# Two transformer layers on one core: u at the phase starts worked out by DVE and ACT alone, with other split points, load queues and buffer counts

## The chip, the core and the metric

The kernel runs on one core of a Trainium2 chip. A core has a matmul engine (TensorE, PE in the profile; its weight loads are PEld), a vector engine (DVE), a scalar engine (ACT), a general one (POOL, GpSimd) and a queue engine (SyncE, SP) that issues most of the DMAs. Each runs its own instructions in the order of its program, and they wait for one another through semaphores. The metric is the device time of one execution in microseconds; less is better.

## What is computed

Two layers act on 128 context tokens and 128 latent tokens with the same weights, in float32, at 1024 channels. Each layer has three phases, and each starts with an RMS norm with a modulation (shift, scale) of its own:

```
u = modulate(rms_norm(x, g[0]), sh1, sc1)
x = x + 0.5 * gt1 * swiglu(u, w_ffn1_in, w_ffn1_out)
u = modulate(rms_norm(x, g[1]), sh2, sc2)
y, ctx_out = token_mixer(u, ...)     # z = u @ w_in: attention, Fourier mixing, mLSTM; gates from u; w_out
x = x + gt2 * y
u = modulate(rms_norm(x, g[2]), sh3, sc3)
x = x + 0.5 * gt3 * swiglu(u, w_ffn2_in, w_ffn2_out)
```

The latent tokens' attention also reads cached keys and values (`cache_k`, `cache_v`), and their mLSTM a cached state (`state_C`). A final norm ends the program. Keys, values and states of the context tokens are outputs too.

## The kernel before

The residual lies in SBUF as `xT`, eight blocks of 128 channels, 256 tokens wide (two groups of 128). A product in float32 is made of three products of rounded halves: `mm3` multiplies `whi` by `uh`, `whi` by `ul` and `wlo` by `uh` (the page's lines 168 to 170). So a weight chunk of 1 MB comes by DMA into one of `N_RAW` raw buffers, on SP's queue, and is split into two units: ACT rounds a unit (`whi`, L1493), DVE subtracts (`wlo`, L1494), into one of `N_SPLIT` split buffers. `pump_split(n)` splits up to n units if a split buffer is free. A raw buffer comes free when both its units are split; then `pump_dma` puts the next load on SP's queue, in the order of the program. A unit of eight blocks is 24 matmuls of 256 columns.

The order of every engine is the order in which the Python program emits instructions (a manual schedule): `steps` are run one after the other, each with its units, then `pump_split`, then what was put into `late`.

Where a phase begins (`first`, used by the mixers and by all FFNs but the very first), four units are multiplied by y = x times scale, which needs no statistics; 1 / rms multiplies the result afterwards. Beside the eight blocks of these products run: `stats` (four small products that sum squares, then the variance on DVE and its power on POOL, L473 and L475), `diag` (1 / rms on a diagonal, `dg`, DVE and ACT), `spread` (a product that spreads it to all partitions, copied to `bcs`), and `apply`, which makes u block by block for all later products:

```
v = vs[k] = t2([P, 256], "v")
(po if k else ve).tensor_mul(v, xT[:, k, :], self.bc)
ac.activation(v[:, G[0]], v[:, G[0]], AF.Identity, scale=self.scale[:, k, 0:1], ...)
ve.tensor_scalar(v[:, G[1]], v[:, G[1]], self.scale[:, k, 1:2], ...)
if k > 0:
    hilo(vs.pop(k - 1), *uk(k - 1))
```

So v is x / rms (POOL for blocks 1 to 7, DVE for block 0, L495); one group is scaled by ACT (L496), the other by DVE (L498); `hilo` rounds the block on ACT (`uh`, L179) and subtracts on DVE (`ul`, L180). `held` has the last two blocks of y, and `warm` loads an ACT table where the phase is an FFN (L520). The four products end in `done`, which reads their PSUM tiles.

In a mixer `loads2` follows directly: it loads cached keys and values (`ckv`) and states (`C0`) on POOL's queue (L695 to L698). The lanes, generators that the steps advance, make attention, gates, mLSTM and Fourier mixing beside the products. The attention lane transposes the cached keys on PE in the middle of the third unit multiplied by u, and swaps parts of q by DMAs on SP's queue (`kl<-q`, L814).

Of the kernel before, what the change touches and what calls it, by code (L numbers as in the profile page):

```python
# [11 lines left out]
F32R = mybir.dt.float32r  # L12
# [5 lines left out]
P = 128  # L18
# [15 lines left out]
N_RAW = 7  # L34
N_SPLIT = 6
# [6 lines left out]
# modulation vectors that each phase works out: those the vector engine sums first, and the others  # L42
# [37 lines left out]
def _pack(inputs):  # L80
    """Short vectors side by side, 128 wide, and the per-head gate biases and stabilisers."""
# [43 lines left out]
def trunk_kernel(ctx: ExitStack, tc: tile.TileContext, a: dict):  # L125
# [58 lines left out]
    # ---------------------------------------------------------------- small inputs  # L184
# [22 lines left out]
    # ---------------------------------------------------------------- persistent  # L207
# [36 lines left out]
    # ---------------------------------------------------------------- start-up  # L244
# [38 lines left out]
    def busy(n):  # L283
        """Products of nothing, which bring the tensor engine to its full clock while it has no data."""
        t = pb([P, 512])
        for _ in range(n):
            mm(t, zeros[:, 0:P], zeros)
# [10 lines left out]
    # ---------------------------------------------------------------- modulation  # L298
    def mod_steps(mods_):
        """Products of some modulation vectors.  # L300

        Four products run side by side: two quarters of the channels, two terms of their sums.
        Vector i takes the rows 2 i and 2 i + 1 of each. The vector engine first sums the channel
        blocks of those of the first list, one term per group, and the products sum its lanes."""
# [88 lines left out]
    # ---------------------------------------------------------------- norms  # L393
    class Norm:
        """Statistics and scaled copies of the residual, block by block.

        y = x * scale goes into the first products of the next phase as it is, with the shift as
        two more columns; 1 / rms multiplies their result. The other products take
        u = y / rms + shift."""

        def __init__(self, scale, shift):
            self.scale, self.shift = scale, shift
            self.y = self.sum = self.last = None
            self.ys = {}
# [58 lines left out]
        def natural(self, x):  # L463
            """Statistics of rows that lie one token to a partition."""
# [23 lines left out]
        def apply(self):  # L488
            U.h = [blk([P, 4, 256], f"uh{i}", F32R) for i in range(2)]
            U.l = [blk([P, 4, 256], f"ul{i}", F32R) for i in range(2)]  # L490
            vs = {}
            for k in range(KD + 1):
                if k < KD:
                    v = vs[k] = t2([P, 256], "v")
                    (po if k else ve).tensor_mul(v, xT[:, k, :], self.bc)  # L495
# [21 lines left out]
    def warm(func):  # L517
        """Has the scalar engine fetch the table of a function before it is needed."""
        if func is not None:
            ac.preload_act_table(func)  # L520

    def first(norm, us, done, func=None):
        """The first four products of a phase, which run while the norm is worked out."""
        ps = first_tiles()
        for k in range(KD):
            first_k(norm.yk, k, us, ps)
            if k == 0:
                norm.stats()
                warm(func)
                held.pop(0)()  # L530
                norm.diag()
                while held:
                    held.pop(0)()
                pump_split(1)
            if k == 1:
                norm.spread()
        norm.apply()
        pump_split(1)
# [7 lines left out]
    def scaled(norm, p_):  # L546
        """A product of y from PSUM times 1 / rms, and its shift, one column per group."""
# [39 lines left out]
    # ---------------------------------------------------------------- FFN  # L587
# [95 lines left out]
    # ---------------------------------------------------------------- mixer  # L683
    def add_mixer(l, norm, norm_next, mods_):
# [7 lines left out]
        def loads2():  # L692
            ac.preload_act_table_set("natural_log_exp_and_others")
            M["ck"] = blk([P, 2, H, P], "ckv")
            po.dma_start(out=M["ck"][:, 0], in_=a["cache_k"][0, l].rearrange("h s d -> s h d"))  # L695
            po.dma_start(out=M["ck"][:, 1], in_=a["cache_v"][0, l].rearrange("h s d -> s h d"))
            M["C0"] = blk([P, 2, H, P], "C0")
            po.dma_start(out=M["C0"], in_=a["state_C"][0, l].rearrange("d h v k -> v d h k"))  # L698
# [95 lines left out]
        # ---- attention  # L794
        def attn_lane():
# [14 lines left out]
            def swap(src):  # L810
                """The halves of each component change places by 32 partitions."""
# [102 lines left out]
            # context  # L914
# [18 lines left out]
            # latent  # L933
# [27 lines left out]
        # ---- Fourier mixing  # L961
        def four_lane():
            """Real input: tokens t and T - t share the cosine part and differ in the sine's sign."""
# [33 lines left out]
        # ---- mLSTM  # L997
        def gate_lane():
# [52 lines left out]
            # rows 4 to 7 of each direction repeat the heads, and carry what rounding leaves of nM  # L1051
# [38 lines left out]
        def mlstm_lane():  # L1090
# [16 lines left out]
            # latent part that comes from the initial memory  # L1107
# [14 lines left out]
            # context state  # L1122
# [97 lines left out]
        # ---- branch products, gates, merge  # L1220
# [83 lines left out]
    def spread_into(lo, hi, mods_):  # L1304
        """Inserts the steps of modulation vectors evenly between two places of the program."""
# [6 lines left out]
    # ---------------------------------------------------------------- program  # L1312
# [6 lines left out]
    def begin(plain_done, st1):  # L1319
        """The first modulation comes one channel block at a time, and the first products with it.  # L1320

        Returns the units of the second pair, of which the first half is used here."""
# [237 lines left out]
```

## Time and profile before

| | before |
|---|---|
| median of 3 runs | 1375.77 us (1375.19 to 1377.95) |
| span of the profiled execution | 1375.9 us |
| PE busy | 1351.3 us, 98% |
| DVE busy | 915.0 us, 67% |
| ACT busy | 682.3 us, 50% |
| POOL busy | 113.0 us, 8% |
| moved from HBM | 297.80 MB, 219 GB/s over the span |
| mean granted clock of TensorE | 0.990 |

The page shows no other time of the profiled execution than its span, which is within the range of the runs. Busy times of engines overlap. A matmul's record lasts some 0.28 us and the next starts about 0.12 us later, so PE's pace is read from start to start. The granted clock is 1.00 for 2.4 GHz and 0.50 for 1.2 GHz.

### The profile page before, as it was taken

Reading aid. Unit: us, or ns where it says so; the run is one execution under the profiler, and the core shown is the slowest. Engines: PE = TensorE matmul, PEld = TensorE weight load, DVE = VectorE, ACT = ScalarE, POOL = GpSimd, SP = SyncE. Lnnn points to the kernel's source line nnn. Section 1 sums busy time; section 2 is a strip of 40 time slices with the busy share of each in tenths; the row PEclk is TensorE's granted clock in tenths of the full one; section 3 lists DMA queues with packets and bytes.
Section 4 is the critical chain, followed back from the end, with each engine's and each line's share of the span. In section 5 each row is a group of like instructions: output and inputs, shape, how many; then the busy total and the mean of one; then the engine's idle time right before and its main releaser. Section 6 shows DMA issues by size and latency. Waiting matters only on the chain.

```text
span 1375.9 us, 26101 instructions
## 1 busy us (share of the span) xinstructions
PE 1351.3 (98%) x10915; PEld 1268.7 (92%) x10916; DVE 915.0 (67%) x1440; ACT 682.3 (50%) x1096; POOL 113.0 (8%) x138
## 2 busy tenths in 40 slices
PE   6999999999999999999999999999999999999998
PEld 4999899888998999999998999998899899999998
DVE  4576755876557589666568666667665668887653
ACT  4544444666544466444455444546564445744442
POOL 2000001300000030000020000130000001200000
PEclk8999999999999999999999999999999999999999
DMA  9999856564468847886639876748445895487520
GB/s 293 333 345 340 260 174 213 159 195 138 157 238 298 272 154 267 300 269 212 206 124 321 305 257 197 204 130 241 154 137 195 297 304 186 147 264 233 192 85 31
DMA packets 247526, 303.68 MB, mean 221 GB/s; under 512 B 5537, under 2 KB 212657, under 8 KB 247409
## 3 DMA queue, kind: packets, MB, share of 16 engines
q1 hardware_dynamic: 245728, 296.98, 66.4%
q0 software_dynamic: 1680, 5.05, 1.1%
q8 instruction: 85, 1.39, 0.4%
q14 instruction: 33, 0.26, 0.1%
HBM read 297.80 MB, written 3.15 MB: 219 GB/s over the span
## 4 chain that ended last, share of the span: by engine, by line
PE 90%; DVE 6%; ACT 2%; DMA 1%; issue 1%; SPq 1%; POOL 0%; ACTq 0%; DVEq 0%
PE pm L168 26%; PE pm L170 25%; PE pm L169 25%; PE pd L165 5%; PE pb L165 2%; DVE wlo L1494 2%; DVE v L498 2%; DVE ul L180 1%; PE pm L752 1%; PE pm L754 1%; PE pm L753 1%; ACT whi L1493 1%; PE pa L165 1%; DMA raw<-w_ada 1%; PE pa L173 1%
## 5 line engine op out<-in xcount | busy, mean ns | idle before, releaser
L1494 DVE TENSOR_TENSOR wlo<-raw,whi 128x1024 fp32r<-128x1024 f32 (+1 forms) x424 | 507.3, 1204 | 326.4 <-ACT whi L1493 316.8
L1493 ACT CAST whi<-raw 128x1024 fp32r<-128x1024 f32 (+1 forms) x424 | 433.9, 1031 | 364.3 <-PE pm L169 253.4
L168 PE MATMUL pm<-uh,whi 128*128 128x256 f32 x1928 | 554.7, 288 | 0.0
L169 PE MATMUL pm<-ul,whi 128*128 128x256 f32 x1928 | 546.8, 284 | 1.7 <-DVE v L498 1.3
L170 PE MATMUL pm<-uh,wlo 128*128 128x256 f32 x1928 | 544.7, 283 | 3.2 <-DVE wlo L1494 3.2
L168 PEld LDWEIGHTS pm<-uh,whi 128*128 128x128 f32 x1928 | 366.8, 190 | 23.7 <-ACT whi L1493 9.1
L170 PEld LDWEIGHTS pm<-uh,wlo 128*128 128x128 f32 x1928 | 366.4, 190 | 4.4 <-DVE wlo L1494 4.4
L169 PEld LDWEIGHTS pm<-ul,whi 128*128 128x128 f32 x1928 | 366.2, 190 | 3.8 <-DVE v L498 1.7
L169 PE MATMUL pm<-hl,whi 128*128 128x256 f32 x704 | 197.9, 281 | 0.0
L168 PE MATMUL pm<-hh,whi 128*128 128x256 f32 x704 | 197.5, 281 | 0.0
L170 PE MATMUL pm<-hh,wlo 128*128 128x256 f32 x704 | 197.5, 281 | 0.0
L168 PEld LDWEIGHTS pm<-hh,whi 128*128 128x128 f32 x704 | 132.8, 189 | 0.0
L170 PEld LDWEIGHTS pm<-hh,wlo 128*128 128x128 f32 x704 | 132.7, 189 | 0.0
L169 PEld LDWEIGHTS pm<-hl,whi 128*128 128x128 f32 x704 | 132.6, 188 | 0.0
L423 POOL TENSOR_TENSOR nsum<-nsum,nsq 128x256 f32<-128x256 f32 x36 | 36.4, 1012 | 833.7 <-ACT nsq L421 833.7
L339 DVE SCALAR_TENSOR_TENSOR acc<-raw,cT,acc 128x512 f32<-128x512 f32 x112 | 78.9, 746 | 0.0
L165 PE MATMUL pd<-raw,cT 128*32 128x512 f32 (+1 forms) x512 | 56.5, 560 | 8.7 <-DMA raw<-w_ada 5.0
L653 ACT ACTIVATE silu<-pm 128x512 f32<-128x512 f32 x39 | 23.3, 597 | 69.5 <-PE pm L170 69.5
L165 PEld LDWEIGHTS pd<-raw,cT 128*32 128x32 f32 x512 | 14.0, 112 | 30.8 <-issue 20.4
L655 DVE TENSOR_TENSOR silu<-silu,pm 128x512 f32<-128x512 f32 x40 | 27.4, 685 | 22.6 <-PE pm L170 22.6
L568 DVE SCALAR_TENSOR_TENSOR xT<-pm,mod,xT 128x128 f32<-128x128 f32 x96 | 28.8, 342 | 18.1 <-PE pm L170 18.0
L1238 ACT ACTIVATE sig<-pm 128x512 f32<-128x512 f32 x24 | 14.4, 598 | 50.3 <-PE pm L170 50.1
(340 smaller groups left out, 1757.8 us busy)
## 6 DMA issues: line engine op xcount, KB each, us to landing
raw<-w_ffn_in SPq DMA_DIRECT2D x88, 1024.0 KB, 7.1
raw<-w_ada SPq DMA_DIRECT2D x64, 1024.0 KB, 6.0
raw<-w_ffn_out SPq DMA_DIRECT2D x32, 1024.0 KB, 7.1
raw<-w_in SPq DMA_DIRECT2D x32, 1024.0 KB, 5.9
raw<-w_branch_gate SPq DMA_DIRECT2D x24, 1024.0 KB, 5.4
raw<-w_ffn_out SPq DMA_DIRECT2D x16, 768.0 KB, 4.8
raw<-w_ada SPq DMA_DIRECT2D x16, 512.0 KB, 7.3
raw<-w_out SPq DMA_DIRECT2D x8, 1024.0 KB, 6.6
```

What stands on the lines that cost most here:

```text
L165: pe.matmul(out, lhsT, rhs, start=start, stop=stop)
L168: pe.matmul(out, sh, mh, start=start, stop=False)
L169: pe.matmul(out, sh, ml, start=False, stop=False)
L170: pe.matmul(out, sl, mh, start=False, stop=stop)
L339: ve.scalar_tensor_tensor(x, w, c, x, op0=ALU.mult, op1=ALU.add)
L423: eng.tensor_add(self.sum, self.sum, sq)
L498: ve.tensor_scalar(v[:, G[1]], v[:, G[1]], self.scale[:, k, 1:2], self.shift[:, k, 1:2], op0=ALU.mult, op1=ALU.add)
L568: ve.scalar_tensor_tensor(xT[:, k, G[g]], ps[:, G[g]], gate[:, k, g:g + 1], xT[:, k, G[g]], op0=ALU.mult, op1=ALU.add)
L653: ac.activation(st["s"], st["a"], AF.Silu)
L655: ve.tensor_mul(st["s"], st["s"], st["g"])
L1493: ac.copy(u.hi, r)
L1494: ve.tensor_sub(u.lo, r, u.hi.bitcast(F32))
```

## The change

- `apply` multiplies by 1 / rms on DVE for all eight blocks, and can be called in two parts: blocks 0 to 4 (with `hilo` up to block 3), then the rest.
- `first` emits `stats` and `diag` after the second block of y products instead of the first, `spread` and `apply` after the third instead of the second and the last. A unit is split ahead of the statistics, and one between the two parts of `apply`.
- The mixers' loads of `ckv` and `C0` are issued by SP instead of POOL.
- `N_SPLIT` is 7 instead of 6, `N_RAW` 6 instead of 7.

```
-N_RAW = 7
-N_SPLIT = 6
+N_RAW = 6
+N_SPLIT = 7
...
-        def apply(self):
-            U.h = [blk([P, 4, 256], f"uh{i}", F32R) for i in range(2)]
-            U.l = [blk([P, 4, 256], f"ul{i}", F32R) for i in range(2)]
-            vs = {}
-            for k in range(KD + 1):
+        def apply(self, k1=KD + 1):
+            if self.at == 0:
+                U.h = [blk([P, 4, 256], f"uh{i}", F32R) for i in range(2)]
+                U.l = [blk([P, 4, 256], f"ul{i}", F32R) for i in range(2)]
+            vs = self.vs
+            ks, self.at = range(self.at, k1), k1
+            for k in ks:
                 if k < KD:
                     v = vs[k] = t2([P, 256], "v")
-                    (po if k else ve).tensor_mul(v, xT[:, k, :], self.bc)
+                    ve.tensor_mul(v, xT[:, k, :], self.bc)
...
             first_k(norm.yk, k, us, ps)
             if k == 0:
-                norm.stats()
                 warm(func)
                 held.pop(0)()
+                pump_split(1)
+            if k == 1:
+                norm.stats()
                 norm.diag()
                 while held:
                     held.pop(0)()
-                pump_split(1)
-            if k == 1:
+            if k == 2:
                 norm.spread()
-        norm.apply()
-        pump_split(1)
+                norm.apply(5)
+                pump_split(1)
+                norm.apply()
+                pump_split(1)
...
-            po.dma_start(out=M["ck"][:, 0], in_=a["cache_k"][0, l].rearrange("h s d -> s h d"))
-            po.dma_start(out=M["ck"][:, 1], in_=a["cache_v"][0, l].rearrange("h s d -> s h d"))
+            nc.sync.dma_start(out=M["ck"][:, 0], in_=a["cache_k"][0, l].rearrange("h s d -> s h d"))
+            nc.sync.dma_start(out=M["ck"][:, 1], in_=a["cache_v"][0, l].rearrange("h s d -> s h d"))
             M["C0"] = blk([P, 2, H, P], "C0")
-            po.dma_start(out=M["C0"], in_=a["state_C"][0, l].rearrange("d h v k -> v d h k"))
+            nc.sync.dma_start(out=M["C0"], in_=a["state_C"][0, l].rearrange("d h v k -> v d h k"))
```

How this moves the instructions, at the start of layer 0's mixer. Numbers behind a name are those of its buffer; lines of the changed kernel are a few higher. DVE before, from the weight split ahead of u on (v_2816 is block 0, v_2820 block 1):

```order
L1494 TENSOR_TENSOR wlo_2721<-raw56_2263,whi_2720 128x1024
L495 TENSOR_TENSOR v_2816<-xT_96,bcs_2738 128x256
L498 TENSOR_SCALAR v_2816<-v_2816,mod0_4_103,mod0_3_102 128x128
L498 TENSOR_SCALAR v_2820<-v_2820,mod0_4_103,mod0_3_102 128x128
L180 TENSOR_TENSOR ul0_2814<-v_2816,uh0_2812 128x256
L498 TENSOR_SCALAR v_2826<-v_2826,mod0_4_103,mod0_3_102 128x128
L180 TENSOR_TENSOR ul0_2814<-v_2820,uh0_2812 128x256
```

DVE in the changed kernel, around the middle of u (v_2782 is block 4, v_2792 block 5):

```order
L498 TENSOR_TENSOR v_2782<-xT_96,bcs_2754 128x256
L501 TENSOR_SCALAR v_2782<-v_2782,mod0_4_103,mod0_3_102 128x128
L180 TENSOR_TENSOR ul0_2758<-v_2776,uh0_2756 128x256
L1500 TENSOR_TENSOR wlo_2789<-raw57_2362,whi_2788 128x1024
L498 TENSOR_TENSOR v_2792<-xT_96,bcs_2754 128x256
L501 TENSOR_SCALAR v_2792<-v_2792,mod0_4_103,mod0_3_102 128x128
L180 TENSOR_TENSOR ul1_2759<-v_2782,uh1_2757 128x256
```

Before, DVE scales and subtracts in turn and multiplies only block 0; now a multiplication stands ahead of each scaling, behind the subtraction of the block before the last, and a `wlo` stands in the middle of u.

ACT before, from the second to last block of y to the copy of 1 / rms (`bcs`):

```order
L435 ACTIVATE y<-xT,mod_4_103 128x128
L179 CAST yh_2103<-y 128x256
L480 ACTIVATE dg<-cst,rstd 128x128
L435 ACTIVATE y<-xT,mod_4_103 128x128
L179 CAST yh_2103<-y 128x256 x2
L1493 CAST whi<-raw_2263 128x1024
L486 COPY bcs<-pb 128x256
```

The same stretch of ACT in the changed kernel:

```order
L435 ACTIVATE y<-xT,mod_4_103 128x128
L179 CAST yh_2107<-y 128x256
L1499 CAST whi<-raw_2291 128x1024
L480 ACTIVATE dg<-cst,rstd 128x128
L435 ACTIVATE y<-xT,mod_4_103 128x128
L179 CAST yh_2107<-y 128x256 x2
L486 COPY bcs<-pb 128x256
```

The weight split has moved from behind the diagonal to ahead of it; on DVE its `wlo` has moved in the same way to a place ahead of the variance. In an FFN the table load stands ahead of all this on ACT, in both kernels.

SP before, where the attention's swap of q comes (`raw` are the weight loads; the loads of `ckv` and `C0` stand on POOL, behind the seven multiplications):

```order
L1471 DMA raw_2868<-w_in 128x8x256
L1471 DMA raw_2878<-w_in 128x8x256
L1471 DMA raw_2913<-w_in 128x8x256
L1471 DMA raw_2993<-w_in 128x4x512
L814 DMA kl<-q 32x4x128 x4
```

SP in the changed kernel:

```order
L1477 DMA raw_2876<-w_in 128x8x256
L1477 DMA raw_2911<-w_in 128x8x256
L701 DMA ckv<-cache_k 128x4x128
L702 DMA ckv<-cache_v 128x4x128
L704 DMA C_2921<-state_C 128x8x128
L1477 DMA raw_2966<-w_in 128x8x256
L1477 DMA raw_3031<-w_in 128x4x512
L820 DMA kl<-q 32x4x128 x4
```

The cached keys, values and states now stand in SP's queue behind `raw_2876`, which waits for the raw buffer of units 7 and 8, and `raw_2911`, which waits for that of units 9 and 10 (the first four units are those of the y products).

## Rows read from the trace of the kernel before

**Rows 1.** Head of the page: the span; engine, busy us, share, instructions.

```profile
span 1375.9 us, 26101 instructions
PE 1351.3 (98%) x10915; PEld 1268.7 (92%) x10916; DVE 915.0 (67%) x1440; ACT 682.3 (50%) x1096; POOL 113.0 (8%) x138
```

**Rows 2.** PE by windows: stretch, length, busy (matmuls), granted clock, DMA share, GB/s.

```profile
720.00:722.00 2.00, 2.00 (x19) 1.00 0.00 0
722.00:724.00 2.00, 1.51 (x11) 1.00 0.03 8
258.00:260.00 2.00, 2.00 (x11) 0.50 0.77 155
262.00:264.00 2.00, 2.00 (x16) 0.84 1.09 350
```

**Rows 3.** Timeline of PE, layer 0's mixer: start, us, instruction, [idle before <-releaser].

```profile
250.69 0.29 PE L168 MATMUL pm<-uh,whi 128*128 128x256 f32 x1
...
257.33 0.58 PE L170 MATMUL pm<-uh,wlo 128*128 128x256 f32 x1 [0.47 <-DVE wlo L1494]
...
263.81 0.60 PE L173 MATMUL pa<-cst,ckv 128*128 128x128 f32 x4
```

**Rows 4.** Timeline of DVE and POOL at the same mixer start.

```profile
244.49 0.96 DVE L495 TENSOR_TENSOR v<-xT,bcs 128x256 f32<-128x256 f32 x1
...
250.43 0.83 POOL L695 DMA_DIRECT2D ckv<-cache_k  x1
...
251.10 1.86 DVE L180 TENSOR_TENSOR ul<-v,uh 128x256 fp32r<-128x256 f32 x1
...
255.09 0.42 DVE L180 TENSOR_TENSOR ul<-v,uh 128x256 fp32r<-128x256 f32 x1 [0.49 <-ACT uh L179]
...
263.51 2.36 DVE L1494 TENSOR_TENSOR wlo<-raw,whi 128x1024 fp32r<-128x1024 f32 x2 [1.08 <-ACT whi L1493]
```

**Rows 5.** Timeline of DVE at the start of layer 1's first FFN.

```profile
709.13 0.16 DVE L473 TENSOR_SCALAR var<-pb 128x2 f32<-128x2 f32 x1 [1.60 <-PE pb L165]
...
712.39 1.23 DVE L1494 TENSOR_TENSOR wlo<-raw,whi 128x1024 fp32r<-128x1024 f32 x1 [0.50 <-ACT whi L1493]
713.53 0.95 DVE L495 TENSOR_TENSOR v<-xT,bcs 128x256 f32<-128x256 f32 x1
...
720.83 0.43 DVE L180 TENSOR_TENSOR ul<-v,uh 128x256 fp32r<-128x256 f32 x1
721.17 0.34 DVE L498 TENSOR_SCALAR v<-v,mod,mod 128x128 f32<-128x128 f32 x1
```

**Rows 6.** Timeline of ACT at the same FFN start.

```profile
708.06 1.28 ACT L520 ACT_TABLE_LOAD   x1
...
711.31 1.05 ACT L1493 CAST whi<-raw 128x1024 fp32r<-128x1024 f32 x1
...
720.01 0.49 ACT L496 ACTIVATE v<-v,mod,mod 128x128 f32<-128x128 f32 x1
720.41 0.39 ACT L179 CAST uh<-v 128x256 fp32r<-128x256 f32 x1
```

**Rows 7.** Timeline of PE at the same FFN start.

```profile
710.86 0.67 PE L165 MATMUL pb<-dg,ones 128*128 128x256 f32 x2 [0.21 <-ACT y L435]
...
720.00 0.28 PE L168 MATMUL pm<-uh,whi 128*128 128x256 f32 x1
...
724.27 0.38 PE L170 MATMUL pm<-uh,wlo 128*128 128x256 f32 x1 [0.76 <-DVE wlo L1494]
```

**Rows 8.** DMA issues of 245 to 275 us: queue, count, KB, us to landing.

```profile
raw<-w_in SPq DMA_DIRECT2D x5, 1024.0 KB, 6.1
...
ckv<-cache_k POOLq DMA_DIRECT2D x1, 256.0 KB, 3.2
...
kl<-q SPq DMA_DIRECT2D x4, 64.0 KB, 5.0
```

**Rows 9.** Timeline of DVE during start-up.

```profile
24.00 2.36 DVE L1494 TENSOR_TENSOR wlo<-raw,whi 128x1024 fp32r<-128x1024 f32 x2 [0.52 <-ACT whi L1493]
```

More of the change, by code (lines that the diff above doesn't have):

```diff
@@ L403, in __init__ @@
             self.y = self.sum = self.last = None
-            self.ys = {}
+            self.ys, self.vs, self.at = {}, {}, 0
         def begin(self):
@@ L533, in first @@
                     held.pop(0)()
+            if k == 2:
+                norm.spread()
+                norm.apply(5)
                 pump_split(1)
-            if k == 1:
-                norm.spread()
-        norm.apply()
-        pump_split(1)
+                norm.apply()
+                pump_split(1)
         def rest():
```

## The prediction

> **What bounds the kernel now.** I read the head of the page first: TensorE (PE) is busy 98% of a span of 1375.9 us [rows 1]. So only PE's gaps can be won back, and whatever makes PE wait longer is paid in full. The profiled execution's span is 0.1 us from the median of the three runs, 1375.77 us, so sums made on the trace carry over unchanged.
>
> Next the timeline of PE where a phase begins. There are five such places that `first` serves: two mixers (near 240 and 909 us) and three FFNs (near 508, 709 and 1177 us). PE runs eight blocks of products of y, which need no statistics, while DVE and ACT work out u; then it turns to products of u. In layer 0's mixer the first product of u starts at 250.69, PE then starves, the second weight's first `wlo` product runs only at 257.33, and PE reaches its look at the cached keys at 263.81 [rows 3]. The windows show the clock beside it: in 258 to 260 us PE is granted 0.50, the lower level of 1.2 GHz, and starts 11 matmuls where a window at full clock, 720 to 722, holds 19; the average is 0.84 in 262 to 264, so the full clock is back at about 262.6, 5.3 us after PE ran steadily again [rows 2]. The second mixer repeats this. In an FFN the gap is smaller: first product of u at 720.00, the second weight's first `wlo` product at 724.27 after one wait of 0.76 us [rows 7].
>
> Then who is late. In the mixer a u subtraction on DVE lasts 1.86 us from 251.10, just as POOL issues the cache loads from 250.43 on [rows 4]. In the FFN nothing of that kind happens; there the weight split queued behind all of u is late.
>
> **The change part by part.** *u without POOL.* Before, POOL multiplies x by 1/rms for seven blocks and runs ahead, so ACT and DVE only finish each block. Now DVE does all eight multiplications, and its order is multiply k, scale k, subtract k-1, multiply k+1. ACT's order is scale k, round k-1 (`uh`). That closes a loop: multiply k+1 stands in DVE's queue behind subtract k-1, that waits for ACT's round k-1, that stands behind ACT's scale k, and that needs multiply k. One turn, from rows without POOL beside them: multiply 0.43 (a DVE operation of the same shape, `ul` at 720.83) [rows 5], 0.03 until ACT starts (as from the end of `uh` at 720.80 to `ul` at 720.83), ACT's scale 0.40 until the round starts (720.01 to 720.41), the round 0.39 [rows 6], 0.03 back, and 0.34 from that subtraction to the next DVE operation (720.83 to 721.17) [rows 5]. That is 1.62 us a block, though DVE itself works only some 0.95 of it.
>
> Now the eight blocks, counted from the start of the first multiply. The first is off the loop and takes 0.7; multiply 1 is at 0.7, 2 at 2.3, 3 at 3.9, 4 at 5.6. Then the weight split in the middle: ACT's `whi` follows round 3 at 6.7 and takes 1.05 [rows 6], DVE's `wlo` starts at 7.8 and lets the next operation start 1.14 later (712.39 to 713.53) [rows 5], so multiply 5 is at 8.95, 6 at 10.6, 7 at 12.2, and the last subtraction ends at 14.2. PE needs a block of u every 0.36 us.
>
> *FFN start.* The table load on ACT (708.06, 1.28 us) [rows 6] stays in front; now a `whi` and its `wlo` stand between it and the statistics. `yh` ends where it did, `whi` runs at about 710.0 to 711.0, `wlo` to 712.2, and only then DVE turns to the variance. From the variance at 709.13 [rows 5] to the spread product at 710.86 [rows 7] it was 1.7 us, some 0.3 of it ACT's other work; so the spread product goes to about 713.6, and PE waits for it some 1.8 us. The y products end at 721.2 instead of 720.0; the first multiply starts at 714.8 instead of 713.53 [rows 5]. u is done at 714.8 + 14.2 = 729.0. PE ends the first weight at 729.4 and reaches the first `wlo` of the second at 729.8, not 724.27: 5.6 us later. From 722 on PE has had three matmuls per 1.6 us, and none for 3 us around the middle split; in the mixer a thinner gap than that took the clock down. I therefore add a stretch at half clock, some 4.7 us more, of which 8 of 19 parts are lost: 2.1. Each FFN start costs 7.7 us, three cost **23.1**.
>
> *Mixer start.* Here no table load stands in front, and the first multiply stays at about 244.4 (now 244.49) [rows 4]; the delays of the variance are what the weight split ahead of that multiply took before. u is done at 258.6, the first weight ends at 259.0, the second, at half clock, takes 24 matmuls of 0.21 us, and half of the third at full clock brings PE to the cached keys at 265.5, against 263.81 [rows 3]: 1.7 us later, POOL's interference being gone.
>
> *Loads from sync.* PE transposes the cached keys in the middle of the third weight, and everything on PE queues behind that. On POOL the load was issued at 250.43 [rows 4] and took 3.2 us [rows 8]. On SP it stands behind two weight loads that wait for raw buffers; the second of them waits for the tenth weight's `wlo`. Before, the first of the pair of `wlo` from 263.51 ends 9.2 us after the last u (255.09 + 0.42) [rows 4]; now one `wlo` fewer stands in front, so 9.2 - 1.15 = 8.05 after 258.6, at 266.65. The weight load takes SP about 0.4, the keys are issued at 267.1. Landing: between 3.2 (the POOL row) and 6.1 (a weight load, one is just ahead); I take 5.0, the row of `kl<-q`, which also follows weights in SP's queue [rows 8]. The keys are there at 272.1. PE stands from 265.5 to 272.1 and is then 8.3 us later than before; clock again, 2.3. Each mixer costs 10.6, both **21.2**. If PE came faster to that point it would only wait longer. The Trainium skill (DMA: Bandwidth & Descriptors, Latency and other measured facts) gives a first byte 0.4 us sooner on the sync path than on GpSimd's; by that rule the sum would be 0.8 us smaller. No row here sets the two apart, since the wait for the queue's turn is longer than either.
>
> *Statistics a block later.* Four small products move behind the second y block; in count nothing changes. The cover of their wait was the first y block; with two it holds unless DVE is held by the split, as in the FFN above.
>
> *7 split, 6 raw buffers.* The kernel holds half a megabyte less in advance. At the phases' start raw buffers are full, and SP waits for them, so I put it at 0. The tight place is start-up, where SP's eighth load now waits for a pair of splits, 24.00 to 26.36 [rows 9]: up to 2.4 us, but a load takes 6.1 us to land [rows 8], so the queue does not run dry meanwhile. The range carries 0 to 2.4.
>
> Sum: 1375.9 + 23.1 + 21.2 = 1420.2, so **1420 us**.
>
> **The rivals.** *A, the loop alone.* The keys land before PE gets there, because SP's wait is shorter than I count or the load overtakes. Then the mixers cost 1.7 each: 1375.9 + 23.1 + 3.4 = 1402 us. Against it: the load stands in program order behind a wait on a `wlo` that itself follows u. For it: a few us decide.
>
> *B, faster.* DVE without POOL beside it is quick: multiplication 0.95 with POOL at work at 713.53, subtraction 0.43 without [rows 5]. If DVE ran at its own pace of 0.95 a block, u would end 8.5 us after the first multiply: at 723.3 in the FFN (no gain, PE's y products end later) and at 252.9 in the mixer, where PE would then be at the keys at 258.1 instead of 263.81, if those have landed. 1375.9 - 2 x 5.7 = 1364.5 us. It decides at about 1.0 us a block. The Trainium skill (SBUF — State Buffer, SBUF: two separate sides) says that DVE and GpSimd share a port pair by an exclusive lock, and the loser "fully blocks"; by that rule B is the outcome. The trace agrees with the lock (0.95 against 0.43); that rule says nothing of the loop through ACT, which those rows do not contain.
>
> *C, no change.* The longer stall is given back by later slack. PE is the bound everywhere else, so there is nothing to give it back.
>
> **How the numbers follow.** Forecast (loop and late keys) 0.60, A 0.27, B 0.08, C 0.02, another slower course 0.03. The low end is A with the turn at 1.45 us and no fall of the clock in the FFNs: 3 x 4.5 + 3.4 gives 1393. The high end is the forecast with the keys at 6.1 or later and 2 us lost at start-up, and with a second DVE delay in the mixers behind it: 1434. Faster by over 0.2% (2.8 us, about what a measurement here can tell from no change) 0.08, within 0.2% 0.03, slower 0.89.
>
> **What would show it.** In the profile after: `v` and `ul` on DVE alternating 1.6 us apart with idle time put down to ACT's `uh`; PE starved for some 6 us at all five starts, the granted clock below 0.9 there also in the FFNs (now 1.00 in 722 to 724 [rows 2]); a wait of PE on DMA for `ckv` at two places, 5 to 7 us long. B would show as DVE back to back and no PE gap. I am wrong if ACT and DVE keep more than one block in flight, or if the key load is issued before the tenth split.

## The result, and the profile after

The changed kernel takes **1427.17 us** (median of 4 runs, 1426.46 to 1429.03) against 1376.76 us of the kernel before beside it: a ratio of **1.0368, 95% interval 1.0354 to 1.0383**, or 50 us more. Its profiled execution spans 1425.6 us, 49.7 more than the one of before. The prediction said 1420 us with a range of 1393 to 1434.

The head of the page of the changed kernel, answering to [rows 1], and PE's longest waits in it (who waited for whom: us in total, times, longest):

```profile
span 1425.6 us, 26112 instructions
PE 1364.2 (96%) x10916; PEld 1279.2 (90%) x10916; DVE 920.0 (65%) x1475; ACT 684.2 (48%) x1096; POOL 79.0 (6%) x97
```

```profile
PE pa L173 <- DMA ckv<-cache_k: 16.3, 2, 9.1
PE pm L168 <- ACT uh L179: 14.7, 15, 2.2
PE pd L165 <- DMA raw<-w_ada: 9.6, 5, 2.4
PE pb L165 <- ACT dg L480: 4.5, 3, 1.5
PE pb L165 <- DVE y L436: 3.4, 2, 1.8
```

POOL has lost 34 us of work and DVE has gained 5. PE's work is the same matmuls, but PE now waits: its idle time (the span less its busy time) has grown from 24.6 to 61.4 us, and the matmuls keep it busy 12.9 us longer, at a mean granted clock of 0.978 instead of 0.990. Two waits for the cached keys are 16.3 us, and fifteen waits for a rounded block of u 14.7 us. The row of `w_ada` is hardly part of the 50 us: 8.4 of its 9.6 us lie ahead of 225 us, where PE waits as long in the kernel before (5.0 us for `w_ada` and 3.7 for a weight split). The last two rows are waits for the diagonal `dg`, which comes later now.

**The loop on DVE and ACT.** Timeline of DVE in layer 0's mixer in the changed kernel (start, us, instruction, idle time before and what ended it), which answers to [rows 4]:

```profile
241.60 1.77 DVE L479 TENSOR_SCALAR dg<-cst,rstd 128x128 f32<-128x128 f32 x1 [0.83 <-POOL rstd L475]
...
244.64 0.43 DVE L498 TENSOR_TENSOR v<-xT,bcs 128x256 f32<-128x256 f32 x1 [0.24 <-ACT bcs L486]
...
246.99 0.42 DVE L498 TENSOR_TENSOR v<-xT,bcs 128x256 f32<-128x256 f32 x1
247.44 0.35 DVE L501 TENSOR_SCALAR v<-v,mod,mod 128x128 f32<-128x128 f32 x1
248.26 0.42 DVE L180 TENSOR_TENSOR ul<-v,uh 128x256 fp32r<-128x256 f32 x1 [0.48 <-ACT uh L179]
248.60 0.42 DVE L498 TENSOR_TENSOR v<-xT,bcs 128x256 f32<-128x256 f32 x1
...
258.10 0.76 DVE L180 TENSOR_TENSOR ul<-v,uh 128x256 fp32r<-128x256 f32 x2 [0.47 <-ACT uh L179]
```

Multiplications start at 246.99 and 248.60, 1.61 us apart, and each subtraction stands 0.47 to 0.48 us for ACT's `uh`. ACT for its part waits for DVE in every turn. Its timeline there:

```profile
247.44 0.49 ACT L499 ACTIVATE v<-v,mod,mod 128x128 f32<-128x128 f32 x1 [0.83 <-DVE v L498]
247.84 0.39 ACT L179 CAST uh<-v 128x256 fp32r<-128x256 f32 x1
```

Neither engine is full; each is the other's wait. The first row of DVE is something else: the diagonal `dg`, 0.29 us long in an FFN start, takes 1.77 us here. I come back to it.

**The late keys.** The timeline of SP, then of PE, in the same mixer; the second answers to [rows 3]:

```profile
267.36 0.57 SPq L701 DMA_DIRECT2D ckv<-cache_k  x1
```

```profile
254.89 0.38 PE L168 MATMUL pm<-uh,whi 128*128 128x256 f32 x1 [2.05 <-ACT uh L179]
...
265.85 0.28 PE L170 MATMUL pm<-uh,wlo 128*128 128x256 f32 x1
273.36 1.09 PE L173 MATMUL pa<-cst,ckv 128*128 128x128 f32 x4 [7.23 <-DMA ckv<-cache_k]
```

PE is ready for the keys at 266.13 and has them 6.0 us after SP issued their load. In the second mixer the wait is 9.1 us.

**The clock.** PE by windows (stretch, length, busy with matmuls, granted clock, DMA share, GB/s): first layer 1's first FFN, where 742 to 744 stands for about 722 to 724 of before [rows 2], then the mixer behind its wait for the keys:

```profile
742.00:744.00 2.00, 0.12 (x2) 1.00 0.03 8
744.00:746.00 2.00, 0.98 (x4) 0.84 0.00 0
746.00:748.00 2.00, 1.64 (x5) 0.50 0.00 0
```

```profile
268.00:272.00 4.00, 0.00 (x0) 0.86 0.95 274
272.00:276.00 4.00, 2.64 (x13) 0.50 1.14 340
```

In the FFN, where the clock stayed at 1.00 before, it now falls to its lower level behind the gap in the middle of u. In the mixer it is down behind that gap, as in the kernel before (0.50 in 260 to 264 us here), is back at 0.99 in 264 to 268, and falls a second time while PE waits for the keys: from the first look at the keys to the first product of `v` the changed kernel takes 6.7 us (273.36 to 280.07), the kernel before 4.7 (263.81 to 268.52), so that fall costs 2.0.

**Where the time went, by phase.** The first product of y starts each phase that `first` serves. From one such start to the next, in us, changed kernel minus before, with the prediction's term beside it:

| phase | before | after | difference | predicted |
|---|---|---|---|---|
| to the first mixer | 237.64 | 236.58 | -1.1 | 0 (0 to 2.4) |
| mixer, layer 0 | 268.03 | 280.66 | +12.6 | +10.6 |
| second FFN, layer 0 | 201.05 | 208.69 | +7.6 | +7.7 |
| first FFN, layer 1 | 200.37 | 208.93 | +8.6 | +7.7 |
| mixer, layer 1 | 267.41 | 281.88 | +14.5 | +10.6 |
| second FFN, layer 1, and end | 201.40 | 208.86 | +7.5 | +7.7 |
| sum | 1375.9 | 1425.6 | +49.7 | +44.3 |

### The profile page after: what moved, and what is told of

Same layout as the page of the kernel before. It is cut to its first block, busy times and chain, and to the rows that moved or that the text cites. A ratio compares the mean times of both kernels' runs of the same rounds, so it can differ in the third digit from the quotient of the medians.

```text
span 1425.6 us, 26112 instructions
## 1 busy us (share of the span) xinstructions
PE 1364.2 (96%) x10916; PEld 1279.2 (90%) x10916; DVE 920.0 (65%) x1475; ACT 684.2 (48%) x1096; POOL 79.0 (6%) x97
## 5 line engine op out<-in xcount | busy, mean ns | idle before, releaser
L168 PE MATMUL pm<-uh,whi 128*128 128x256 f32 x1928 | 560.2, 291 | 14.7 <-ACT uh L179 14.7
L168 PEld LDWEIGHTS pm<-uh,whi 128*128 128x128 f32 x1928 | 371.4, 193 | 40.3 <-ACT uh L179 18.1
L169 PEld LDWEIGHTS pm<-ul,whi 128*128 128x128 f32 x1928 | 370.6, 192 | 3.9 <-DVE ul L180 3.5
L170 PEld LDWEIGHTS pm<-uh,wlo 128*128 128x128 f32 x1928 | 371.0, 192 | 1.3 <-DVE wlo L1500 1.3
L423 POOL TENSOR_TENSOR nsum<-nsum,nsq 128x256 f32<-128x256 f32 x36 | 39.4, 1093 | 873.6 <-issue 462.9
L165 PEld LDWEIGHTS pd<-raw,cT 128*32 128x32 f32 x512 | 13.5, 109 | 31.1 <-issue 12.9
L758 PE MATMUL pm<-whi,uh 128*128 128x512 f32 x96 | 39.2, 408 | 0.0
```

The costliest lines, as they stand in the source:

```text
L165: pe.matmul(out, lhsT, rhs, start=start, stop=stop)
L168: pe.matmul(out, sh, mh, start=start, stop=False)
L169: pe.matmul(out, sh, ml, start=False, stop=False)
L170: pe.matmul(out, sl, mh, start=False, stop=stop)
L423: eng.tensor_add(self.sum, self.sum, sq)
L758: pe.matmul(ps[g], xh[:, G[g]], wh, start=(k == 0), stop=False)
```

## The experiments: the four parts one by one

The theory at this point: two costs, DVE's loop with ACT and the late keys, and nothing from the order or the buffers. Its rivals: that the keys are late only because the loop is slow, that the order in the phase's start is the cost, or that the smaller stock of raw buffers is. Four kernels put one part of the change each into the kernel before.

**Loads on SP alone.** In `loads2`, thrice:

```
-            po.dma_start(out=M["ck"][:, 0], ...
+            nc.sync.dma_start(out=M["ck"][:, 0], ...
```

> The kernel before with the mixers' three loads on SP, nothing else. Late keys: the load stands behind the first wlo that ends at 264.66 us in layer 0, is issued near 265.1 and lands 6.0 us later at 271.1; PE, without POOL's interference, is there near 262.3, waits 8.8, is 7.3 us later than before, and loses 2.0 more to the clock: 9.3 each, 1376 + 18.6 = 1394 us. Rival, only the slow loop makes the keys late: 1373 to 1377 us.

Measured 1398.4 us (1396.88 to 1399.97), ratio 1.0152, interval 1.0130 to 1.0173: 21 us more. The keys are late without any loop. PE's waits:

```profile
PE pa L173 <- DMA ckv<-cache_k: 22.1, 2, 11.4
```

The size was under-estimated because the waits were 10.8 and 11.4 us, not 8.8. In layer 0, counted from the phase's start, PE came 0.5 us sooner than expected, the load was issued 1.2 us later, and it landed after 6.2 us instead of 6.0. The late issue follows a stall of DVE, since POOL's interference did not go with the loads. Without them POOL's clearing of `zgh` and `zgl` moves up beside DVE's work on u. POOL, then DVE, in that kernel's first mixer:

```profile
248.62 0.80 POOL L700 MEMSET zgh<- 128x832 f32 x1
249.35 0.79 POOL L701 MEMSET zgl<- 128x832 f32 x1
```

```profile
248.00 2.88 DVE L498 TENSOR_SCALAR v<-v,mod,mod 128x128 f32<-128x128 f32 x1
```

An operation of 0.34 us lasts 2.88 and ends at 250.88, when POOL is through with these and three smaller clears (250.79).

**DVE multiplying alone.** In `apply`:

```
-                    (po if k else ve).tensor_mul(v, xT[:, k, :], self.bc)
+                    ve.tensor_mul(v, xT[:, k, :], self.bc)
```

> The kernel before with DVE making all eight multiplications, nothing else. Loop: 1.62 us a block, u done 13.05 us after the first multiplication, and the next weight split 1.7 us behind it. FFN: second weight's first wlo product near 728.3 instead of 724.27, and 2 us of half clock: 6 each; mixers some 2 each: 1376 + 22 = 1398 us. Rival, DVE alone is quick (0.43 us a multiplication), the loop is a matter of the new order: 1373 to 1379 us.

Measured 1395.31 us (1391.92 to 1396.22), ratio 1.0131, interval 1.0108 to 1.0155: 18 us more, where 22 were expected. DVE's multiplications in layer 0's mixer:

```profile
246.77 0.42 DVE L495 TENSOR_TENSOR v<-xT,bcs 128x256 f32<-128x256 f32 x1
...
248.38 0.42 DVE L495 TENSOR_TENSOR v<-xT,bcs 128x256 f32<-128x256 f32 x1
```

They are 1.61 us apart, so the loop needs nothing else of the change. By phase the FFNs cost 4.2, 5.6 and 3.9 us, the mixers 1.1 and 1.0.

**The new order alone.** The diff of `first` and of `apply` as in the change, with POOL's multiplication, loads and buffers of before.

> The kernel before with the new order of the phase's start alone: a weight split ahead of the statistics, the statistics a block later, a split in the middle of u; POOL multiplies, buffers and loads as before. Loop and late keys: the spread product 1.4 us late in the FFNs, 4 us in all, and up to 1 us gained in each mixer since the second weight is ready when u is: 1376 + 2 = 1378 us, within 1374 to 1381. Rival, the order is the cost at the FFN starts: 1390 us or more.

Measured 1377.41 us (10 runs, 1375.56 to 1378.62), ratio 1.0001, interval 0.9992 to 1.0010: nothing. It is not nothing everywhere: each FFN is 1.2 to 1.4 us longer, since PE waits 1.5 us there for the late diagonal, and each mixer is shorter, by 0.9 and 2.8. In layer 0's mixer PE is at the keys at 258.92 instead of 263.81, 3.4 us of it gained since the phase began, but most of that is given back 35 us later. The first row is PE's wait for the attention lane's `pc` in the kernel before, the second that in this one:

```profile
298.31 1.11 PE L173 MATMUL pa<-cst,pc 128*128 128x128 f32 x4 [0.57 <-DVE pc L865]
```

```profile
294.44 1.12 PE L173 MATMUL pa<-cst,pc 128*128 128x128 f32 x4 [1.50 <-DVE pc L871]
```

Two windows around it show PE busy 2.50 of 4 us in 292 to 296 and then a granted clock of 0.61 in 296 to 300, where the kernel before stands at 1.00:

```profile
292.00:296.00 4.00, 2.50 (x17) 0.96 0.67 232
296.00:300.00 4.00, 4.00 (x24) 0.61 0.45 132
```

**The buffers alone.** `N_RAW = 6`, `N_SPLIT = 7`.

> The kernel before with 7 split and 6 raw buffers, nothing else. Buffers at nothing: 0.9 us gained at start-up and up to 1.4 us lost where the modulations of layer 1's first FFN wait for their weights: 1375 to 1378 us. Rival, the shorter queue of raw buffers makes PE wait for weights: 1380 us or more.

Measured 1388.39 us (1386.42 to 1389.86), ratio 1.0078, interval 1.0056 to 1.0100: **11 us more**, so the rival's time came true and the theory fell at this point. PE's waits for a modulation's weights are 15.5 us in this kernel, but 8.4 of them are at start-up, as in the changed kernel. What is new are two waits of 3.5 us, in layer 0's second FFN and in layer 1's first, where the kernel before has none. The one in layer 0:

```profile
530.43 1.94 PE L165 MATMUL pd<-raw,cT 128*32 128x512 f32 x8 [3.51 <-DMA raw<-w_ada]
```

Four parts alone make 21 + 18 + 0 + 11 = 50 us, as much as the whole change. That is partly luck, for phase by phase it is not a plain sum. From the profiled executions, us against the kernel before (the one of "DVE multiplies" is the fastest of its four runs, 3.4 us below their median):

| phase | SP loads | DVE multiplies | order | buffers | sum of four | whole change |
|---|---|---|---|---|---|---|
| mixer, layer 0 | +10.0 | +1.1 | -0.9 | +1.7 | +11.9 | +12.6 |
| second FFN, layer 0 | 0.0 | +4.2 | +1.2 | +3.9 | +9.3 | +7.6 |
| first FFN, layer 1 | -0.1 | +5.6 | +1.2 | +3.9 | +10.5 | +8.6 |
| mixer, layer 1 | +10.2 | +1.0 | -2.8 | +1.4 | +9.7 | +14.5 |
| second FFN, layer 1 | +0.7 | +3.9 | +1.4 | 0.0 | +6.0 | +7.5 |

In the two FFNs where a modulation's weights come late, the loop hides part of that: while PE starves for u, the weights land, and PE's waits for them there are 0 and 1.2 us in the changed kernel instead of 3.5 each. In the second mixer the whole costs 4.7 us more than its parts. The keys are not the reason: with the loads back on POOL (below) that mixer is still 5.4 us longer than before, where the other three parts alone sum to -0.4. Why these three cost more together stays open.

## Why the buffers cost

Six raw buffers mean one load fewer under way. Seven split buffers do something less plain. The order of SP's loads is worked out from due places, and a weight of the FFN is due `N_SPLIT` units ahead of its use, a modulation's weight at its own place. With seven, one more FFN weight goes ahead of the modulation's. SP's queue in layer 0, before, and with 7 and 6:

```profile
459.87 20.95 SPq L1471 DMA_DIRECT2D raw<-w_ffn_in  x5
488.76 0.37 SPq L1471 DMA_DIRECT2D raw<-w_ada  x1
492.06 0.37 SPq L1471 DMA_DIRECT2D raw<-w_ffn_in  x1
501.46 3.04 SPq L1471 DMA_DIRECT2D raw<-w_ada  x2
```

```profile
460.88 31.41 SPq L1471 DMA_DIRECT2D raw<-w_ffn_in  x6
499.81 0.37 SPq L1471 DMA_DIRECT2D raw<-w_ada  x1
502.49 0.37 SPq L1471 DMA_DIRECT2D raw<-w_ffn_in  x1
513.67 12.12 SPq L1471 DMA_DIRECT2D raw<-w_ada  x2
```

Six FFN weights instead of five stand ahead, and the last of the pair of `w_ada` leaves at about 525.4 (513.67 + 12.12, less 0.37) instead of 504.1. Which of the two numbers does it? 7 split with 7 raw buffers was not tried; two kernels tell it apart otherwise. The first has `N_RAW = 6` alone:

> The kernel before with 6 raw buffers instead of 7, split buffers at 6. It tells why the 7 split and 6 raw buffers together cost 11 us (PE waits 3.5 us for a modulation's weights at two FFN starts, and 1.1 us of half clock behind each). Raw theory, one weight load fewer under way is what makes them late: 1386 to 1389 us. Order theory, the seventh split buffer lets a weight of the FFN be due one place sooner and so puts it ahead of the modulation's weights in SP's queue: 1376 to 1380 us.

Measured 1379.94 us (10 runs, 1377.28 to 1382.30), ratio 1.0029, interval 1.0019 to 1.0039: 4 us. Its trace has the same waits for a modulation's weights, shorter: 1.6 us in layer 0's second FFN and 1.1 in layer 1's first. The second keeps 7 and 6 buffers and mends the due place alone:

```
-            at = max(0, len(units) - N_SPLIT) if u.split else len(units)
+            at = max(0, len(units) - 6) if u.split else len(units)
```

> The kernel before with 7 split and 6 raw buffers, but the order of SP's weight loads still worked out as if there were 6 split buffers. Order theory: the modulations' weights are back in their place, 1376 to 1380 us. Raw theory: as with both changed, 1386 to 1389 us. If this and the run with 6 raw buffers alone both stand near 1382, each does half.

Measured 1376.84 us (10 runs, 1374.87 to 1378.98), ratio 1.0003, interval 0.9994 to 1.0012: the 11 us are gone, with the same 7 and 6 buffers. In SP's queue five FFN weights stand ahead of the first `w_ada` again:

```profile
459.13 28.11 SPq L1471 DMA_DIRECT2D raw<-w_ffn_in  x5
490.18 0.37 SPq L1471 DMA_DIRECT2D raw<-w_ada  x1
```

The last of the pair of `w_ada` behind it leaves at about 511.9 there, between the 504.1 and the 525.4 of the other two, and PE's two waits of 3.5 us are gone. So 7 split and 6 raw buffers together cost nothing measurable; the order of loads that follows from the 7 costs 11 us. One raw buffer less costs 4 us by itself. That a seventh split buffer takes these 4 away, once the due place is mended, fits a split that is made sooner and so gives its raw buffer back sooner; that reading was not tested by itself.

## The experiments: the change with one part undone

Four kernels take one cost out of the changed kernel.

**Loads back on POOL.**

```
-            nc.sync.dma_start(out=M["ck"][:, 0], ...
+            po.dma_start(out=M["ck"][:, 0], ...
```

> The changed kernel with the mixers' three loads issued from POOL again, all else as changed. Loop and late keys (two separate costs): PE's two waits on the cached keys, 7.2 and 9.1 us, go, and with them the half clock behind each, 2.0 and 1.8 us by the shifts of PE's products: 1427 - 20 = 1407 us. Rival, POOL's descriptors hold up DVE's loop as they held one subtraction in the kernel before (1.86 instead of 0.43 us), once or twice a mixer: 1410 to 1413 us. Rival, the wait for the keys only covers another one (weights not yet split): PE waits for that instead, 1420 us or more.

Measured 1408.15 us (1406.61 to 1410.09), ratio to before 1.0230, interval 1.0215 to 1.0246. No wait for the keys is left: 19 us of the 50 were the place of three DMAs. DVE stalls in the mixer, as the second expectation had it, but mainly during POOL's memsets: it lasts from 244.87 to 247.35, while POOL issues the loads from 242.65 to 245.08. POOL, then DVE:

```profile
245.07 0.81 POOL L706 MEMSET zgh<- 128x832 f32 x1
245.80 0.81 POOL L707 MEMSET zgl<- 128x832 f32 x1
```

```profile
242.72 0.29 DVE L479 TENSOR_SCALAR dg<-cst,rstd 128x128 f32<-128x128 f32 x1 [0.83 <-POOL rstd L475]
...
244.87 2.48 DVE L501 TENSOR_SCALAR v<-v,mod,mod 128x128 f32<-128x128 f32 x1
```

Here the diagonal is quick, 0.29 us, since POOL's memsets come after it.

**Loads on SP, but ahead of the phase's weights.** The three loads leave `loads2` and stand at the head of `first`:

```
         ps = first_tiles()
+        if keys is not None:
+            keys()
```

> The changed kernel with the three loads still on SP, but issued ahead of the three weight loads that the phase's start puts in SP's queue. Late keys by place in the queue: they are issued near 240 instead of 267 us, PE's two waits and the half clock behind them go, 1407 us. Rival, SP itself is slow or the memory is: the keys land when they did, 1427 us. Rival, the three loads (1 MB) push the weights back: PE waits for a weight split instead, 1415 us or more.

Measured 1410.62 us (1409.88 to 1412.02), ratio 1.0249, interval 1.0233 to 1.0264: 17 us less than the changed kernel, within 4 us of what was expected, and no wait for the keys. SP issues the load 36 us sooner:

```profile
231.23 0.50 SPq L702 DMA_DIRECT2D ckv<-cache_k  x1
```

So it was the place in SP's queue, not SP as such.

**POOL multiplying again.**

```
-                    ve.tensor_mul(v, xT[:, k, :], self.bc)
+                    (po if k else ve).tensor_mul(v, xT[:, k, :], self.bc)
```

> The changed kernel with POOL multiplying seven blocks again, all else as changed. Loop theory: the three FFN starts fall from 7.3 us to the 1.4 us by which the spread product is late, 17 us less; in the mixers u, the splits behind it and so the keys' issue come 3.2 us sooner, 6.4 us less: 1403 us. Rival, it is the order in the phase's start (a weight split ahead of the statistics and one in the middle) and not the multiplying engine that costs: 1421 us or more. Shown by DVE's multiplications no longer 1.62 us apart and no idle time put down to ACT's rounding.

Measured 1406.13 us (1403.57 to 1407.31), ratio 1.0212, interval 1.0197 to 1.0228: 21 us less than the changed kernel, where 24 were expected. PE's waits for `uh` fall out of the list; those for the keys grow to 19.9 us, as PE comes sooner, and those for the modulations' weights are back in the two FFNs, with 2.4 and 2.7 us.

**DVE multiplying, one block ahead.** The multiplication of block k + 1 stands ahead of the subtraction of block k - 1, not behind it, so the ring is open:

```
-                    v = vs[k] = t2([P, 256], "v")
-                    ve.tensor_mul(v, xT[:, k, :], self.bc)
+                    for m in range(k + (k > 0), min(k + 2, KD)):
+                        vs[m] = t2([P, 256], "v")
+                        ve.tensor_mul(vs[m], xT[:, m, :], self.bc)
+                    v = vs[k]
```

> The changed kernel, DVE still multiplying, but each block's multiplication written one block sooner, so that it no longer stands behind the subtraction that waits for ACT. Loop theory: the turn falls from 1.62 us to DVE's own sum, 0.46 + 0.27 + 0.35 = 1.1 us; u is done some 10.6 instead of 14.2 us after the first multiplication; the FFNs lose 3.6 us each and most of the 2 us of half clock, the mixers 3.6 each: 1403 to 1409 us. Rival, DVE's work and not the order of it makes the 1.62 us: 1427 us within 2.

Measured 1403.96 us (1402.49 to 1405.90), ratio 1.0196, interval 1.0179 to 1.0213: 23 us less, about as much as POOL's return. DVE in layer 0's mixer has no idle time left between blocks, and a turn is 0.92 us, less than the 1.1 expected:

```profile
247.91 0.42 DVE L499 TENSOR_TENSOR v<-xT,bcs 128x256 f32<-128x256 f32 x1
248.24 0.34 DVE L503 TENSOR_SCALAR v<-v,mod,mod 128x128 f32<-128x128 f32 x1
248.50 0.41 DVE L180 TENSOR_TENSOR ul<-v,uh 128x256 fp32r<-128x256 f32 x1
248.83 0.42 DVE L499 TENSOR_TENSOR v<-xT,bcs 128x256 f32<-128x256 f32 x1
```

The same operations on the same engine, in another order, take 0.92 instead of 1.62 us a block: the loop is shown.

## All three mended

**The change with its three faults mended**: one block ahead, loads early, 6 split and 7 raw buffers; u without POOL, the middle split and the later statistics stay.

> The changed kernel with three things mended: each multiplication of DVE written one block sooner, the three loads on SP ahead of the phase's weights, 6 split and 7 raw buffers. Kept: u without POOL, the split in the middle, the statistics a block later. If the three costs are all there is: 1427 - 23 - 17 - 11 = 1376 us, within 1372 to 1380. Rival, a cost of its own remains in making u on DVE (1.1 us a block against PE's 0.36): 1385 us or more.

Measured 1374.78 us (11 runs, 1374.42 to 1378.25), ratio to before 0.9990, interval 0.9981 to 0.9999. The three costs are all there is, as far as these runs can tell: without them the kernel is 52 us faster than the changed one and stands within 1 us of the kernel before. Two of PE's longest waits in it:

```profile
PE pb L165 <- ACT dg L480: 4.6, 3, 1.5
PE pb L165 <- DVE y L436: 3.6, 2, 1.8
```

They are the late diagonal of the new order: 1.5 us in each FFN start and, behind POOL's memsets, 1.8 in each mixer.

**The kernel before with two parts of the change**: the middle split, POOL multiplying, statistics where they were, and the early loads on SP.

> The kernel before with POOL multiplying and its own order of statistics, plus the split in the middle of u and the three loads on SP ahead of the phase's weights. PE's wait for the second weight at the FFN starts (0.8 us and some starved products) goes, 1 us each; in the mixers u and the second weight come 4 us sooner, of which most is given back at the attention lane's wait for DVE, as with the new order alone: 1371 to 1375 us. Rival, all is given back: 1376 to 1378 us.

Measured 1374.04 us (11 runs, 1372.73 to 1376.80), ratio 0.9989, interval 0.9980 to 0.9998. The medians of both lie a tenth of a per cent below the kernel before, less than the 0.2% that a comparison here safely tells. By its trace PE is at the keys at 259.09 instead of 263.81, and the attention lane's wait for DVE takes part of that back, as with the order alone.

## The prediction, step by step

**The loop: right.** 1.62 us a block was worked out from rows without it; the trace has 1.61 to 1.62. u done 14.2 us after the first multiplication: 258.86 - 244.64 = 14.22. In layer 1's first FFN, 19.2 us later than before when it begins, y's products were to end at 721.2 + 19.2 = 740.4 and the first product of u starts at 740.5; the second weight's first `wlo` product was to run at 749.0 and runs at 749.64; the fall of the clock came as said. 7.7 a phase against 7.6, 8.6 and 7.5. (A slip in the sum: 4.7 x 8 / 19 is 2.0, not 2.1; the total moves by 0.3.) The 0.9 us by which the middle one is over stand beside a wait of PE of 1.16 us for a modulation's weights (at 755.70), which the sum put at nothing.

**The late keys: mechanism right, size short.** All times in the mixer are 1.1 us earlier than in the kernel before when it starts. The issue was put at 267.1, or 266.0 with that, and came at 267.36; the landing was put at 5.0 us and took 6.0. Together PE had the keys 2.3 us later than the sum had them. 1.0 is the landing: of the three rows offered in [rows 8] the nearest was the 1 MB weight just ahead in the same queue (6.1), not the small `kl<-q`. 1.3 is the step "the first multiply stays at about 244.4": on that clock it would be 243.3, and it came at 244.64. (It did come at 244.42 in the kernel with the loads back on POOL, whose phase starts at 237.7, as in the kernel before, and whose diagonal is quick.) What was missed is what POOL does with the time it is given. Relieved of its multiplications and loads it clears `zgh` and `zgl` at once, beside DVE's diagonal, which then takes 1.77 us, and everything on DVE is behind. "POOL's interference being gone" was the wrong sentence: it was moved.

The half clock behind the keys was put at 2.3 and cost 2.0. The second mixer costs 14.5, not the 12.6 of the first: of the 1.8 more, 1.35 lie ahead of its first look at the keys (its load took about 0.8 longer to land) and 0.1 in the half clock; the rest stays open.

**Statistics a block later: right that it is nothing in sum**, by two sides that cancel, -3.7 in the mixers and +3.8 in the FFNs by the table of parts; the FFN's side was in the 7.7.

**Buffers at nothing: wrong**, 11 us alone. The sum asked whether the queue runs dry and looked for the answer at the phases' start and at start-up. What the number also sets is the order of the loads, and that stands in one line of the executor. In the whole change it shows only in part, because a PE that starves for u gives the weights time (the table of parts): the last FFN, where no modulation waits, costs 7.5 by loop and order alone, and the other two hardly more. With POOL multiplying again those two are still 3.8 and 4.1 us longer than before, the last one 1.8. Mended of the other two costs, the kernel would have paid it: 1427 - 23 - 17 = 1387 us, a sum of single runs and not itself a run, against the 1375 measured with 6 split and 7 raw. That difference, 12 us, is about the price of the buffers alone. At start-up nothing can be told: profiles of kernels with the same start-up code differ by 1 to 2 us there, and the kernel before's was a late one.

**The rivals.** A, the loop without late keys, was put at 1402; the two kernels that remove the lateness stand 6 and 9 us above it, at 1408 and 1411, and in the change itself its condition was not met. B's rate, 0.95 a block, is what DVE does (0.92) as soon as the order lets it, but B's time is not: with all three mended the rate is there and the keys are early, and the kernel takes 1375 us, not 1364.5. By phase its mixers are 3.2 and 1.9 us shorter than before, where B had 5.7 each, and its FFNs 0.1 to 1.5 us longer. C gave nothing back.

So the total came out 7 us short. 5.4 of it are in the profiled executions: mixers short by 2.0 and 3.9, the middle FFN by 0.9, less 1.1 at start-up and 0.3 in the other FFNs; the rest is the step "sums made on the trace carry over unchanged". Each run of the changed kernel takes 1.7 to 1.8 us longer than its span (1427.35 and 1425.6 in the profiled one). That span and median stood together in the kernel before was luck, if its profiled execution was, as its late start-up suggests, a slow one.

## What to carry over

When an operation moves to another engine, write out both engines' queues and look for a closed ring of waits: here multiply, scale, round and subtract cost 1.62 us a block in one order and 0.92 in another. A DMA that moves to another queue gets that queue's place in line, so find what stands ahead of it and what that waits for. A count of buffers may also be a term in the order of loads: read where the name is used before putting it at nothing.

## What the runs showed of the hardware

DVE's `TENSOR_SCALAR` of 128 x 128 is long where POOL clears two tiles of 128 x 832 and some smaller ones beside it: 1.77 us in the changed kernel, 2.48 with the loads on POOL and 2.88 with the loads alone moved, where it otherwise takes 0.29 to 0.35. A subtraction of two operands beside such a memset, at 253.49 in the kernel before, took its usual 0.43:

```profile
253.49 0.43 DVE L180 TENSOR_TENSOR ul<-v,uh 128x256 fp32r<-128x256 f32 x1 [0.46 <-ACT uh L179]
```

```profile
253.70 0.78 POOL L701 MEMSET zgl<- 128x832 f32 x1
```

The Trainium skill (SBUF — State Buffer, SBUF: two separate sides) says that the loser "fully blocks", and that a DVE operation with two SBUF inputs is held only by a POOL operation that reads SBUF. These rows agree with both: a memset's row names no input. The page's other condition is a mode of DVE that no row here shows, and no run moved the memsets alone, so the cause is read from rows, not shown by a change. In the kernel before, it was again a `TENSOR_SCALAR` that stood beside POOL's issue of the loads:

```profile
250.83 2.13 DVE L498 TENSOR_SCALAR v<-v,mod,mod 128x128 f32<-128x128 f32 x1
```

The subtraction at 251.10 [rows 4], which the prediction read as the slow one, stands behind it on DVE, and both end at 252.96. So memsets are not the only work of POOL beside which this happens.

The loads of 256 KB (cached keys and values) took 3.2 to 3.6 us to land on POOL's queue in the kernel before and 5.2 to 6.5 in the kernel with the loads back on POOL; on SP they took 6.0 to 6.7 in the changed kernel and 6.3 to 7.9 with all three mended. So the queue alone does not set it. In the first two kernels the DMA share was 0.03 from 250 to 252 us and 1.01 from 244 to 246, just behind the issue; that this traffic is the cause is not shown. The 0.4 us by which the Trainium skill (DMA: Bandwidth & Descriptors, Latency and other measured facts) has the first byte sooner on the sync path can't be seen under that spread.
